# Eleven gate/up tiles by seven products, in pairs, with two weight sums made by accumulating transfers

## The chip, the cores and the metric

The kernel runs on one core of a Trainium2 chip. The metric is the time of one execution in device microseconds; the kernel before takes 910.9 us (median of three runs, 910.83 to 911.63). The engines are named as the profile names them: PE (TensorE, matrix products), PEld (its weight loads), DVE (VectorE), ACT (ScalarE), POOL (GpSimd) and SP (SyncE, which issues transfers here).

## The reference

One encoder layer over 512 positions of width 1024, in float32: a layer norm, two attention branches and their output projection, a memory cross-attention, and a convolutional gated linear unit, each followed by a layer norm. The change lies in the last of these:

```python
def conv_glu(h, w_gate, w_up, conv_w, conv_b, w_down):
    s = h.shape[1]
    g = h @ w_gate                       # (512, 1024) @ (1024, 2816)
    half = CONV_WIDTH // 2               # CONV_WIDTH = 3
    gp = jnp.pad(g, ((0, 0), (half, half), (0, 0)))
    g = sum(gp[:, j:j + s] * conv_w[j] for j in range(CONV_WIDTH)) + conv_b
    return (jax.nn.gelu(g, approximate=False) * (h @ w_up)) @ w_down
```

## The kernel before

Every matrix product in the kernel is made of three in a reduced format: each float32 operand is split into a rounded part, hi (an ACT cast), and the remainder, lo (a DVE subtraction), and hi·hi, hi·lo and lo·hi are summed in PSUM.

**The gate/up stage.** The 2816 columns of w_gate and w_up are cut into 22 tiles of 128 columns. A tile f yields 128 features of the gate and 128 of the up projection for all 512 positions. The activations h2T lie transposed, 8 blocks of 128 along the contraction. Tiles 0 and 1 are computed while the stage before ends. From tile 2 on there are two kinds:

- An *ordinary* tile loads the two 512 KB weight tiles (`w_cols`, L144), splits each into hi and lo, and runs `gemm_fm` (L170) twice: 2 x 8 x 3 matmuls of 128x512, gate into a PSUM tile g, up into s.
- A *seven-product* tile (`seven`, L1424; the tiles named in SEVEN, L52) takes gate and up together as a 2x2 block matrix, with gate and up as its rows and the two halves of the contraction as its columns (a11, a12 of the gate; a21, a22 of up), and the activations as four quarters B11 to B22 (contraction halves by halves of the positions). In Winograd's form of Strassen's method it needs seven products of blocks in place of eight: 7 x 4 x 3 = 84 matmuls of 128x256. For this it makes four sums of weight blocks on DVE (s1 to s4, L1433 to L1437), four remainders and as many casts (`parts`, L1417), and puts the products together afterwards with one ACT copy and four DVE additions (L1458 to L1462). The sums of the activations' quarters (T, by `t_forms`, L1388) are made once, during tiles 2 to 4.

`ffn_tail` (L1350) then applies the convolution's three taps, the Gelu and the product with up, into act[f]. After tile 21 the down projection runs over act.

**Buffers.** Weights as loaded lie in "raw" (3 buffers of 512 KB). s1 and s3 share one tile, s2 and s4 another, of "gb" (2 buffers). hi and lo have 6 buffers each; a seven-product tile takes four of each, an ordinary one two. A seven-product tile's output is put together in gu, which has 1 buffer. In PSUM, t and o have one buffer each (tile f's first product goes into o for odd f, into t for even f), g and s two each; a seven-product tile takes both g and one s, an ordinary one one g and one s.

**Order.** On PE the matmuls of this stage are issued in the order of the program text (`tc.manual_schedule`, L1466); on the other engines a planner places the instructions by a simulation of their times, and each engine's queue then runs in that order. Weight loads are issued by SP. Before the change POOL issues no transfers; in this stage it has nothing to do.

Seven-product tiles are 5, 7, 9, 11, 13, 15, 17 and 19, so that an ordinary tile stands behind each.

Of the kernel before, what the change touches and what calls it, by code (L numbers as in the profile page):

```python
# [9 lines left out]
F32 = mybir.dt.float32  # L10
# [3 lines left out]
ALU = mybir.AluOpType  # L14
# [3 lines left out]
P = 128  # L18
D = 1024
S = 512  # L20
NB = S // P
KD = D // P
# [26 lines left out]
]  # L49

MEM_AT = (2, 0)
SEVEN = (5, 7, 9, 11, 13, 15, 17, 19)  # L52
WARM = (12, 3)
CI, CF, CS, CMA, CM1, CM3 = 0, 128, 129, 130, 514, 770
CW = 898
# [17 lines left out]
def hymba_layer(ctx: ExitStack, tc: tile.TileContext, A, cst_d, out):  # L73
    nc = tc.nc
    X = mybir.AxisListType.X

    def pool(name, bufs=1, side="left", space=None):
        kw = {} if space is None else {"space": space}
        if space is None:
            kw["side"] = side  # L80
        return tc.tile_pool(name=name, bufs=bufs, **kw)

    cpool = ctx.enter_context(pool("const", side="right"))
    wpool = ctx.enter_context(pool("weights", side="right"))
# [110 lines left out]
    def ps_tile(tag, bufs, shape=None):  # L195
        return gpool.tile(shape or [P, 512], F32, tag=tag, bufs=bufs, name=tag)

    def g_tile():
        return ps_tile("g", 2)

    def s_tile():
        return ps_tile("s", 2, [P, 2, 512])
# [1123 lines left out]
    act = fp.tile([P, NF, S], F32, name="act")  # L1326
# [20 lines left out]
        for i in range(4):  # L1347
            pre_gemm(i, 1)

    def ffn_tail(f, pg, pu):  # L1350
        c = fp.tile([P, S], F32, tag="c", bufs=3, name="c")
        nc.scalar.activation(c, pg, AF.Identity, scale=cwT[:, 22 + f : 23 + f], bias=cwT[:, 66 + f : 67 + f])
        nc.vector.scalar_tensor_tensor(
            c[:, 1:S], pg[:, 0 : S - 1], cwT[:, f : f + 1], c[:, 1:S], ALU.mult, ALU.add
        )
        nc.vector.scalar_tensor_tensor(
            c[:, 0 : S - 1], pg[:, 1:S], cwT[:, 44 + f : 45 + f], c[:, 0 : S - 1], ALU.mult, ALU.add
        )
        nc.scalar.activation(c, c, AF.Gelu)
        nc.vector.tensor_tensor(act[:, f, :], c, pu, ALU.mult)  # L1360

    HT, HK = S // 2, KD // 2
# [4 lines left out]
    R12, R22 = (raw_u[:, HK * i : HK * (i + 1), sr] for i in range(2))  # L1369
# [3 lines left out]
    def two_k(v, i):  # L1373
        return v[:, 2 * i : 2 * i + 2]

    def t_parts(n, i, r):
        if n < 3:
            hl = [xpool.tile([P, 2, HT], F32R, tag="x", bufs=12, name="x") for _ in range(2)]
        else:
            hl = [two_k(t4, i), cpool.tile([P, 2, HT], F32R, tag="rope", bufs=2, name="t4l")]  # L1380
        nc.scalar.copy(hl[0], r)
        nc.vector.tensor_tensor(hl[1], r, hl[0].bitcast(F32), ALU.subtract)
        T.setdefault(n, []).append(hl)

    def t_tile():
        return fp.tile([P, 2, HT], F32, tag="c", bufs=3, name="r")

    def t_forms(j):  # L1388

        if j == 2:  # L1390
            for i in range(2):
                r = t_tile()
                nc.vector.tensor_tensor(r, two_k(R22, i), two_k(R12, i), ALU.subtract)
                t_parts(2, i, r)
            return
        r, q = t_tile(), t_tile()
        for t, B in ((r, B11), (q, B21)):
            nc.vector.tensor_tensor(t, two_k(B[0], j).bitcast(F32), two_k(B[1], j).bitcast(F32), ALU.add)
        nc.vector.tensor_tensor(r, two_k(R12, j), r, ALU.subtract)
        t_parts(0, j, r)  # L1400
        nc.vector.tensor_tensor(r, two_k(R22, j), r, ALU.subtract)
        t_parts(1, j, r)
        nc.vector.tensor_tensor(q, q, r, ALU.subtract)
        t_parts(3, j, q)

    def moving(n):
        return lambda w, k: T[n][k // 2][w][:, k % 2, :]

    def quarter(q):
        return lambda w, k: q[w][:, k, :]  # L1410

    def product(ps, wt, u):
        for k in range(HK):
            for a, b in ((0, 0), (0, 1), (1, 0)):
                mm(ps, wt[a][:, k, :], u(b, k), k + a + b == 0, k == HK - 1 and a == 1)

    def parts(raw, n):  # L1417
        hi = wpool.tile([P, n, P], F32R, tag="hi", bufs=6, name="hi")
        nc.scalar.copy(hi, raw)
        lo = wpool.tile([P, n, P], F32R, tag="lo", bufs=6, name="lo")  # L1420
        nc.vector.tensor_tensor(lo, raw, hi.bitcast(F32), ALU.subtract)
        return [[t[:, HK * i : HK * (i + 1), :] for t in (hi, lo)] for i in range(n // HK)]

    def seven(f):  # L1424
        raw = []
        for name in ("w_gate", "w_up"):
            raw.append(wpool.tile([P, KD, P], F32, tag="raw", bufs=3, name="raw"))
            nc.sync.dma_start(raw[-1], A[name][0].rearrange("(k p) f -> p k f", p=P)[:, :, f * P : (f + 1) * P])
        a11, a12, a21, a22 = (t[:, HK * i : HK * (i + 1), :] for t in raw for i in range(2))
        s13, s24 = (wpool.tile([P, KD, P], F32, tag="gb", bufs=2, name="gb") for _ in range(2))  # L1430
        s1, s3, s2, s4 = (t[:, HK * i : HK * (i + 1), :] for t in (s13, s24) for i in range(2))
        A11, A12 = parts(raw[0], KD)
        nc.vector.tensor_tensor(s1, a21, a22, ALU.add)  # L1433
        nc.vector.tensor_tensor(s3, a11, a21, ALU.subtract)
        S1, S3 = parts(s13, KD)
        nc.vector.tensor_tensor(s2, s1, a11, ALU.subtract)
        nc.vector.tensor_tensor(s4, a12, s2, ALU.subtract)  # L1437
        S2, S4 = parts(s24, KD)
        (A22,) = parts(a22, HK)
        p1_ = ps_tile(("t", "o")[f % 2], 1)[:, sl]  # L1440
        product(p1_, A11, quarter(B11))
        two = [g_tile(), g_tile(), s_tile()[:, 0, :]]
        product(two[0][:, sl], A12, quarter(B21))
        product(two[1][:, sl], S1, moving(0))
        product(two[1][:, sr], S3, moving(2))
        product(two[0][:, sr], S2, moving(1))
        product(two[2][:, sl], S4, quarter(B22))
        product(two[2][:, sr], A22, moving(3))
        gu = fp.tile([P, 2 * S], F32, tag="gu", bufs=1, name="gu")
        u34 = act[:, f, :]  # L1450

        def twice(v):
            return v.unsqueeze(1).to_broadcast([P, 2, HT])

        def pair(v):
            return v.rearrange("p (a t) -> p a t", a=2)

        nc.scalar.copy(gu[:, S + HT :], p1_)  # L1458
        nc.vector.tensor_tensor(pair(gu[:, 0:S]), pair(two[0]), twice(gu[:, S + HT :]), ALU.add)
        nc.vector.tensor_tensor(pair(u34), pair(two[1]), twice(gu[:, sr]), ALU.add)  # L1460
        nc.vector.tensor_tensor(gu[:, S + HT :], two[1][:, sl], u34[:, sr], ALU.add)
        nc.vector.tensor_tensor(gu[:, HT : S + HT], two[2], u34, ALU.add)  # L1462
        ffn_tail(f, gu[:, 0:S], gu[:, S:])

    pin()
    with tc.manual_schedule(engines={nc.tensor.engine}):  # L1466
        for f in range(2):
            ffn_tail(f, pre[2 * f][1], pre[2 * f + 1][1])
        for f in range(2, NF):
            if f in SEVEN:  # L1470
                seven(f)
                continue
            wg = w_cols(A["w_gate"][0], f * P)
            wu = w_cols(A["w_up"][0], f * P)
            pg = g_tile()
            pu = s_tile()[:, 0, :]
            gemm_fm(pg, wg, h2T, 0, S)
            gemm_fm(pu, wu, h2T, 0, S)
            ffn_tail(f, pg, pu)
            if f < 5:  # L1480
                t_forms(f - 2)
# [78 lines left out]
```

## Time and profile before

| | |
|---|---|
| median of 3 runs | 910.9 us (910.83 to 911.63) |
| profiled execution, its own time | 911.27 us |
| its span, first to last instruction | 909.5 us |
| mean granted clock of TensorE | 0.998 |
| gate/up tiles 5 to 21 | 603.4 to 782.1 us of the span |
| HBM read / written | 87.82 MB / 4.19 MB |

The profile is of one execution. Busy times are sums of instruction durations per engine; matmuls overlap their neighbours, so that a matmul of 128x512 shows 0.39 us while the next starts 0.23 us after it. In the groups of instructions a row names line, engine, operation, output<-inputs and shapes; behind the bar stand the busy time, the mean of one in ns, and the idle time of the engine just before them with what ended it. In the timeline a row begins with its start and duration in us.

### The profile page before, as it was taken

To read this page: it belongs to the slowest core of one execution; us is meant where nothing else is said; L and a number is where in the kernel's file an instruction comes from. 1 tells how busy PE (TensorE), PEld (TensorE's weight loads), DVE (VectorE), ACT (ScalarE), POOL (GpSimd) and SP (SyncE) were. 2 spreads that over 40 slices of the span, in tenths; PEclk is the share of its full clock that TensorE was granted. 3 is DMA by queue.
4 is the path that set the end of the run, shared out by engine and by line. 5 is a ranking of instruction groups with operands and counts; after the bars stand their busy time and mean duration, and the time that the engine had idled before them with its cause. 6 is when DMAs were issued, how large, how long until landed. Compare 5 with 4: busy or idle time off the path is not lost.

```text
span 909.5 us, 12905 instructions
## 1 busy us (share of the span) xinstructions
PE 896.6 (99%) x5097; PEld 768.3 (84%) x5097; DVE 560.2 (62%) x956; ACT 385.0 (42%) x672; POOL 127.2 (14%) x106
## 2 busy tenths in 40 slices
PE   9999999999999999999999999999999999999996
PEld 7778987898878798788988889799999999888885
DVE  7975146335446667869466576877777767433346
ACT  4563436415545576315454224344444345222210
POOL 1064033431443420010000010000000000000001
PEclk9999999999999999999999999999999999999999
DMA  6762041214221337316222304233333354223201
GB/s 220 225 213 70 24 139 47 73 67 117 70 70 47 93 117 233 138 46 171 85 70 70 93 25 129 82 93 93 95 114 94 96 160 140 93 93 103 83 23 70
DMA packets 116942, 92.84 MB, mean 102 GB/s; under 512 B 12472, under 2 KB 100752, under 8 KB 116882
## 3 DMA queue, kind: packets, MB, share of 16 engines
q1 hardware_dynamic: 116048, 89.80, 32.4%
q10 hardware_dynamic: 834, 2.22, 0.6%
q8 instruction: 40, 0.66, 0.3%
q14 instruction: 20, 0.16, 0.1%
HBM read 87.82 MB, written 4.19 MB: 101 GB/s over the span
## 4 chain that ended last, share of the span: by engine, by line
PE 95%; DVE 3%; ACT 1%; DMA 1%; issue 0%; POOL 0%; DVEq 0%; ACTq 0%
PE g L168 54%; PE s L168 24%; PE o L168 5%; PE t L168 4%; PE o L694 3%; PE s L682 2%; PE s L208 1%; DMA vt<-in_ln_in_g_dram 1%; PE s L1225 0%; DVE lo L282 0%; DVE oA L348 0%; DVE st L312 0%; DVE Tlo L367 0%; POOL zs L530 0%; DVE mx L1206 0%
## 5 line engine op out<-in xcount | busy, mean ns | idle before, releaser
L138 DVE TENSOR_TENSOR lo<-raw,hi 128x1024 fp32r<-128x1024 f32 x126 | 157.2, 1249 | 86.6 <-ACT hi L136 85.9
L136 ACT CAST hi<-raw 128x1024 fp32r<-128x1024 f32 x126 | 132.3, 1051 | 141.5 <-PE g L168 92.5
L168 PE MATMUL g<-Thi,hi 128*128 128x512 f32 x240 | 94.8, 395 | 0.0
L168 PE MATMUL g<-Tlo,hi 128*128 128x512 f32 x240 | 94.2, 393 | 0.0
L168 PE MATMUL g<-Thi,lo 128*128 128x512 f32 x240 | 94.0, 392 | 0.0
L109 POOL TENSOR_TENSOR rs<-ve,mhalf 128x1 f32<-128x1 f32 x18 | 15.3, 852 | 524.9 <-DVE ve L115 513.6
L530 POOL TENSOR_TENSOR zs<-zs,rsn 128x512 f32<-128x512 f32 x29 | 59.2, 2040 | 147.5 <-DVE zs L529 147.5
L168 PE MATMUL g<-Uhi,hi 128*128 128x512 f32 (+1 forms) x224 | 77.5, 346 | 1.0 <-ACT hi L136 1.0
L168 PE MATMUL g<-Ulo,hi 128*128 128x512 f32 (+1 forms) x224 | 77.1, 344 | 0.0
L168 PE MATMUL g<-Uhi,lo 128*128 128x512 f32 (+1 forms) x224 | 77.0, 344 | 0.0
L168 PE MATMUL g<-hi,Thi 128*128 128x512 f32 x184 | 71.6, 399 | 0.0
L168 PE MATMUL g<-hi,Tlo 128*128 128x512 f32 x184 | 70.9, 395 | 0.5 <-DVE Tlo L1173 0.5
L168 PE MATMUL g<-lo,Thi 128*128 128x512 f32 x184 | 70.7, 395 | 0.4 <-DVE lo L282 0.4
L528 DVE TENSOR_TENSOR zs<-g,rc 128x512 f32<-128x512 f32 x29 | 20.0, 689 | 68.2 <-PE g L168 31.6
L168 PE MATMUL g<-x,hi 128*128 128x256 f32 x320 | 58.8, 284 | 0.0
L168 PEld LDWEIGHTS g<-Thi,hi 128*128 128x128 f32 x240 | 45.1, 188 | 11.1 <-issue 0.9
L168 PEld LDWEIGHTS g<-Tlo,hi 128*128 128x128 f32 x240 | 45.1, 188 | 10.3 <-issue 1.4
L168 PEld LDWEIGHTS g<-Thi,lo 128*128 128x128 f32 x240 | 45.1, 188 | 9.3
L168 PEld LDWEIGHTS g<-x,hi 128*128 128x128 f32 x320 | 50.0, 192 | 0.5 <-issue 0.3
L168 PEld LDWEIGHTS g<-hi,Tlo 128*128 128x128 f32 x184 | 42.2, 230 | 6.4 <-DVE Tlo L1173 1.0
L168 PEld LDWEIGHTS g<-Uhi,hi 128*128 128x128 f32 x224 | 42.5, 190 | 5.8 <-ACT hi L136 1.2
L138 DVE TENSOR_TENSOR lo<-act,hi 128x512 fp32r<-128x512 f32 x22 | 14.8, 690 | 52.8 <-ACT hi L136 52.8
(363 smaller groups left out, 2091.8 us busy)
## 6 DMA issues: line engine op xcount, KB each, us to landing
raw<-in_w_in_dram SPq DMA_DIRECT2D x37, 512.0 KB, 3.8
raw<-in_w_gate_dram SPq DMA_DIRECT2D x22, 512.0 KB, 3.8
raw<-in_w_up_dram SPq DMA_DIRECT2D x22, 512.0 KB, 3.9
raw<-in_w_down_dram SPq DMA_DIRECT2D x22, 512.0 KB, 3.4
raw<-in_w_xk_dram SPq DMA_DIRECT2D x8, 512.0 KB, 3.9
raw<-in_w_xv_dram SPq DMA_DIRECT2D x8, 512.0 KB, 3.5
raw<-in_w_xq_dram SPq DMA_DIRECT2D x8, 512.0 KB, 4.6
raw<-in_w_xo_dram SPq DMA_DIRECT2D x8, 512.0 KB, 3.5
```

The source lines that it names most:

```text
L109: nc.gpsimd.tensor_tensor(out_, in_, mhalf, ALU.pow)
L136: nc.scalar.copy(hi, raw)
L138: (eng or nc.vector).tensor_tensor(lo, raw, hi.bitcast(F32), ALU.subtract)
L168: on_pe(nc.tensor.matmul(o, l, r, start=first, stop=last))
L208: on_pe(nc.tensor.transpose(ps[:, i // 4, f : f + P], t[:, i * P : (i + 1) * P], ident))
L528: nc.vector.tensor_tensor(zc, ps, rc, ALU.mult)
L530: nc.gpsimd.tensor_tensor(sh, sh, rsn, ALU.mult)
L682: nc.tensor.transpose(tp[:, k, :], s_, ident)
L694: nc.tensor.matmul(o[HJ[j], t0:t1], lhs(j), rhs(j), start=i == 0, stop=i == len(parts) - 1)
```

## The change

Eleven tiles become seven-product tiles: 5, 7, 8, 10, 11, 13, 14, 16, 17, 19 and 20. Five pairs of them stand one behind the other.

In such a tile two of the four weight sums are no longer made on DVE. SP loads a quarter (4 blocks of 128x128, 256 KB) straight into the place of s1 and another into that of s3, and POOL issues a transfer for each that adds the first half of w_up onto it in memory (`accum_op=ALU.add`): s1 = a22 + a21, s3 = a11 + a21. The whole raw tiles of gate and up are loaded as before; the half a21 of the raw up tile is then not used. [...]

```diff
-SEVEN = (5, 7, 9, 11, 13, 15, 17, 19)
+SEVEN = (5, 7, 8, 10, 11, 13, 14, 16, 17, 19, 20)
...
-    def ffn_tail(f, pg, pu):
+    def ffn_tail(f, pg, pu, sign=1):
...
-        nc.vector.tensor_tensor(act[:, f, :], c, pu, ALU.mult)
+        if sign == 1:
+            nc.vector.tensor_tensor(act[:, f, :], c, pu, ALU.mult)
+        else:
+            nc.vector.scalar_tensor_tensor(act[:, f, :], c, -1.0, pu, ALU.mult, ALU.mult)
...
-        nc.vector.tensor_tensor(r, two_k(R12, j), r, ALU.subtract)
+        nc.vector.tensor_tensor(r, r, two_k(R12, j), ALU.subtract)
         t_parts(0, j, r)
-        nc.vector.tensor_tensor(r, two_k(R22, j), r, ALU.subtract)
+        nc.vector.scalar_tensor_tensor(r, r, -1.0, two_k(R22, j), ALU.mult, ALU.subtract)
         t_parts(1, j, r)
-        nc.vector.tensor_tensor(q, q, r, ALU.subtract)
+        nc.vector.scalar_tensor_tensor(q, r, -1.0, q, ALU.mult, ALU.subtract)
         t_parts(3, j, q)
...
     def seven(f):
+        s13, s24 = (wpool.tile([P, KD, P], F32, tag="gb", bufs=2, name="gb") for _ in range(2))
+        s1, s3, s2, s4 = (t[:, HK * i : HK * (i + 1), :] for t in (s13, s24) for i in range(2))
+
+        def rows_of(name, i):
+            return A[name][0].rearrange("(k p) f -> p k f", p=P)[:, HK * i : HK * (i + 1), f * P : (f + 1) * P]
+
+        for t, name, i in ((s1, "w_up", 1), (s3, "w_gate", 0)):
+            nc.sync.dma_start(t, rows_of(name, i))
+            nc.gpsimd.dma_start(t, rows_of("w_up", 0), accum_op=ALU.add)
         raw = []
...
-        a11, a12, a21, a22 = (t[:, HK * i : HK * (i + 1), :] for t in raw for i in range(2))
-        s13, s24 = (wpool.tile([P, KD, P], F32, tag="gb", bufs=2, name="gb") for _ in range(2))
-        s1, s3, s2, s4 = (t[:, HK * i : HK * (i + 1), :] for t in (s13, s24) for i in range(2))
+        a11, a12, _, a22 = (t[:, HK * i : HK * (i + 1), :] for t in raw for i in range(2))
         A11, A12 = parts(raw[0], KD)
-        nc.vector.tensor_tensor(s1, a21, a22, ALU.add)
-        nc.vector.tensor_tensor(s3, a11, a21, ALU.subtract)
+        nc.vector.tensor_tensor(s2, s1, a11, ALU.add)
+        nc.vector.tensor_tensor(s4, a12, s2, ALU.add)
         S1, S3 = parts(s13, KD)
-        nc.vector.tensor_tensor(s2, s1, a11, ALU.subtract)
-        nc.vector.tensor_tensor(s4, a12, s2, ALU.subtract)
         S2, S4 = parts(s24, KD)
...
-        ffn_tail(f, gu[:, 0:S], gu[:, S:])
+        ffn_tail(f, gu[:, 0:S], gu[:, S:], -1)
```

## The prediction

> **What bounds the kernel now.** I read the page first: its busy times, then its chain of work.
>
> ```profile
> span 909.5 us, 12905 instructions
> ...
> PE 896.6 (99%) x5097; PEld 768.3 (84%) x5097; DVE 560.2 (62%) x956; ACT 385.0 (42%) x672; POOL 127.2 (14%) x106
> ...
> PE 95%; DVE 3%; ACT 1%; DMA 1%; issue 0%; POOL 0%; DVEq 0%; ACTq 0%
> ```
>
> TensorE is busy for 99% of the span and makes 95% of the chain that ended last. A busy PE is not PE at its peak, so the next view is who PE waited for, from 556 us (the end of the stage before) to the end of the span. Its only row is one wait of 1.0 us, before any seven-product tile:
>
> ```profile
> PE g L168 <- ACT hi L136: 1.0, 1, 1.0
> ```
>
> So in the gate/up stage matmuls follow one another without a gap, and the stage is as long as its matmuls. What one tile costs is read from the chain in order of time, over one seven-product tile (tile 7: its matmuls into o, g, s) and the ordinary tile 8 behind it (into g, s), and from the windows over the same two tiles. A window row gives busy times of PE, weight load, DVE, ACT and POOL, then granted clock, DMA share and GB/s.
>
> ```profile
> 624.53 1.43 PE o L168 x12
> 625.97 5.76 PE g L168 x48
> 631.73 2.88 PE s L168 x24
> 634.61 5.47 PE g L168 x24
> 640.08 5.44 PE s L168 x24
> 645.51 0.12 PE o L168
> 624.37:634.45 10.08, 10.08 (x86) 10.07 (x85) 8.16 (x11) 4.56 (x5) 0.00 (x0) 1.00 0.37 106
> 634.45:645.35 10.90, 10.90 (x50) 9.01 (x49) 7.31 (x10) 4.45 (x7) 0.00 (x0) 1.00 0.32 96
> ```
>
> Tile 7 runs from 624.53 to 634.61, 10.08 us; tile 8 from there to 645.51, 10.90 us. The granted clock is 1.00 in both. DVE has 8.16 of 10.08 and 7.31 of 10.90 us, 74% of the two. It is the engine nearest to becoming a bound.
>
> **The change part by part.**
>
> *Three more tiles in seven products.* SEVEN grows from 8 to 11 of the 17 tiles from 5 to 21. Each swap replaces 10.90 us of matmuls by 10.08 us: 0.82 us, times 3 = 2.46 us. This lies wholly on the path. It is the only gain there is, since everything else that the change removes is DVE time, for which PE does not wait today.
>
> *Pairs.* Until now an ordinary tile, light on DVE, stood behind every seven-product tile. Now two heavy tiles stand together five times (7-8 to 19-20), then one ordinary tile. So the DVE bill of such a tile decides. These are groups of instructions (count, busy us, mean ns, then idle before them) between 603.39 and 782 us, and last ACT's copy in the view of the tile gu (min, median and max ns):
>
> ```profile
> L1433 DVE TENSOR_TENSOR gb<-raw 128x512 f32<-128x512 f32 x7 | 4.8, 692 | 15.3 <-DMA raw<-in_w_up_dram 15.3
> L1436 DVE TENSOR_TENSOR gb<-gb,raw 128x512 f32<-128x512 f32 x7 | 4.8, 685 | 0.0
> L1434 DVE TENSOR_TENSOR gb<-raw 128x512 f32<-128x512 f32 x7 | 4.8, 684 | 0.0
> L1437 DVE TENSOR_TENSOR gb<-raw,gb 128x512 f32<-128x512 f32 x7 | 4.8, 684 | 0.0
> L138 DVE TENSOR_TENSOR lo<-raw,hi 128x1024 fp32r<-128x1024 f32 x22 | 26.8, 1222 | 13.0 <-ACT hi L136 12.9
> L1421 DVE TENSOR_TENSOR lo<-gb,hi 128x1024 fp32r<-128x1024 f32 x14 | 17.2, 1226 | 8.7 <-ACT hi L1419 8.7
> L1421 DVE TENSOR_TENSOR lo<-raw,hi 128x512 fp32r<-128x512 f32 x7 | 4.8, 681 | 0.0
> L1459 DVE TENSOR_TENSOR gu<-g,gu 128x512 f32<-128x512 f32 x8 | 5.5, 683 | 0.0
> L1460 DVE TENSOR_TENSOR act<-g,gu 128x512 f32<-128x512 f32 x8 | 5.5, 691 | 0.2
> L1461 DVE TENSOR_TENSOR gu<-g,act 128x256 f32<-128x256 f32 x8 | 3.3, 417 | 0.0
> L1462 DVE TENSOR_TENSOR gu<-s,act 128x512 f32<-128x512 f32 x8 | 5.4, 681 | 0.0
> L1353 DVE SCALAR_TENSOR_TENSOR c<-gu,cwT,c 128x511 f32<-128x511 f32 x8 | 6.0, 751 | 3.0 <-ACT c L1352 3.0
> L1360 DVE TENSOR_TENSOR act<-c,gu 128x512 f32<-128x512 f32 x8 | 5.5, 691 | 5.3 <-ACT c L1359 5.3
> L1458 ACT COPY gu<-o x8: 372/372/373, 605.0 to 751.9; 128x256 f32<-128x256 f32 x8
> ```
>
> Per seven-product tile: four weight sums, 0.69 + 0.68 + 0.69 + 0.68 = 2.74; three whole remainders (lo) of 1.22 or 1.23 and a half one of 0.68, 4.35; four recombinations, 0.68 + 0.69 + 0.42 + 0.68 = 2.47; two taps of 0.75 and the product 0.69, 2.19. Together 11.75 us, more than the tile's 10.08. The change takes L1433 and L1434 away (-1.38) and turns the last product into the form of L1353 (0.75 for 0.69, +0.06): 10.43 us. An ordinary tile costs 2 x 1.22 + 2 x 0.75 + 0.69 = 4.63. Three tiles cost 2 x 10.43 + 4.63 = 25.5 of 31.06 us, 82%; without the accumulating transfers it would be 91%. So DVE keeps up over a period, if not inside a pair; what carries a pair is that weights are made ahead. Two of the three sign changes in the prepared forms of the activations also go from 0.69 to 0.75, four instructions in tiles 2 and 3, 0.24 us; PE has no wait on DVE there, so I cost them at nothing (uncovered: 0.24).
>
> *Handover inside a pair.* gu has one buffer: tile 8's first recombination needs ACT's copy into it, which waits for tile 7's last reader, L1360. Tile 7's end on DVE today:
>
> ```profile
> 635.31 0.42 DVE L1461 TENSOR_TENSOR gu<-g,act 128x256 f32<-128x256 f32 x1
> 635.65 0.68 DVE L1462 TENSOR_TENSOR gu<-s,act 128x512 f32<-128x512 f32 x1
> 636.25 0.68 DVE L1421 TENSOR_TENSOR lo<-raw,hi 128x512 fp32r<-128x512 f32 x1
> 639.51 0.69 DVE L1360 TENSOR_TENSOR act<-c,gu 128x512 f32<-128x512 f32 x1 [0.76 <-ACT c L1359]
> ```
>
> L1360 ends at 640.20, 5.59 us into the next tile. Add the copy (0.37) and L1459 (0.68): 6.64. The deadline is the tile behind the pair, which writes that g buffer at 10.08. Spare: 3.4 us. Queued in front on DVE today, from the start of tile 8, are one whole and one half remainder (1.9). In a pair, as the six hi/lo buffers come free, it would be at most three whole ones and two sums (3 x 1.22 + 2 x 0.69 = 5.0), 3.1 more. It just fits, so I take nothing. The other deadline, L1461 of tile 7 before tile 8's third product (2.88 us in, at 637.49 on this clock), has 1.8 us to spare over its end at 635.73.
>
> *Accumulating transfers.* Each seven-product tile gets two plain 256 KB loads on SP and two accumulating 256 KB transfers on POOL. POOL's queue is empty there: its last instruction before the stage and the first after it are the rows below. The trace shows no accumulating transfer and none issued by POOL, so its time is bounded.
>
> ```profile
> raw<-in_w_up_dram SPq DMA_DIRECT2D x14, 512.0 KB, 3.9
> gb<-in_ln_g_dram SPq DMA_DIRECT2D x1, 512.0 KB, 5.2
> 552.04 0.92 POOL L109 TENSOR_TENSOR rs<-ve,mhalf 128x1 f32<-128x1 f32 x1 [11.27 <-DVE ve L115]
> 880.57 0.91 POOL L109 TENSOR_TENSOR rs<-ve,mhalf 128x1 f32<-128x1 f32 x1 [327.61 <-DVE ve L115]
> L530 POOL TENSOR_TENSOR zs<-zs,rsn 128x512 f32<-128x512 f32 x29 | 59.2, 2040 | 147.5 <-DVE zs L529 147.5
> 621.25 0.37 SPq L1428 DMA_DIRECT2D raw<-in_w_up_dram  x1
> ```
>
> Below: 3.9 us, a plain load of twice the size. Above: two such loads (destination and source are both read) and 2.0 us of POOL's work, its dearest row, 9.8. I take 5.2, the slowest transfer into the same gb buffers. What can wait: for tile 10 the first load goes out when the buffer of tile 8's sums comes free, about 2.4 us into tile 7 (ACT cast and lo after tile 6 has ended). With 3.9 for the load, the sum is whole 6.3 us in plus the transfer. The add that reads it (L1436) holds what is behind it in DVE's queue, tile 7's L1462 to L1360 at worst: 4.55 us (635.65 to 640.20) which must end 9.0 into tile 8, so it must start by 14.5 us into tile 7; two adds before it leave 13.1. So a transfer may take 6.8 us at no cost; 5.2 costs nothing.
>
> The Trainium skill, "DMA: Bandwidth & Descriptors", section "Anatomy of one DMA — SWDGE (gpsimd) path", gives 2.0 us plus the bytes over 436 GB/s for a transfer issued by GpSimd; for 256 KB that is an estimate of 2.6 us, and by it the sum would stay at -2.46. No run here shows it yet.
>
> SP issues four transfers where it issued two, 0.37 us each, and a load that waits for a gb buffer holds the raw loads behind it. The row of 621.25 is for tile 9, which starts at 645.51: 24 us ahead, so a few us there cost nothing. The DMA engines: 0.37 of 10.08 us is 3.7 us per tile now; half as much again for the two plain loads and as much once or twice over for the two accumulating ones make 7.4 to 9.3, and 18 to 22 of 31 us over three tiles. No limit.
>
> Sum: -2.46 us. The profiled execution took 911.27 us, of which the span is 909.5; it would become 908.8. The median shown is 910.9, 0.37 lower, so **908.4**.
>
> **The rivals.**
>
> *Handover pays* (chance 0.28). If DVE also waits for ACT between the remainders put in front (today it idles 0.3 to 1.0 us before one), 3.1 becomes 3.4 to 4.1 against 3.4 spare, some 0.4 us in each of five pairs: +2.0, 910.4. For: DVE's 10.43 us in a 10.08 us tile. Against: the chain of L1462 to L1360 has its own gaps, in which remainders fit. A new POOL queue that adds up to the 1.8 us that now lie outside the span ends here too. Bounds 909.1 to 912.7.
>
> *The accumulating transfer is late* (0.18). It decides from 6.8 us on. Each us beyond stops PE in four places (a pair with a pair to come), break-even 2.46 / 4 = 0.6, at 7.4. At 9.8 it is 3.0 x 4 = 12 us, 920.4; halfway, at 8.3, 6 us, 914.4. For: DVE already stands still for a plain load in the row of L1433, 15.3 us in 7 times. Against: 24 us of lead.
>
> *POOL's issue is held off by DVE* (0.04). Today DVE runs without a gap from 604.08 to 609.45:
>
> ```profile
> 604.08 0.69 DVE L1433 TENSOR_TENSOR gb<-raw 128x512 f32<-128x512 f32 x1 [1.32 <-DMA raw<-in_w_up_dram]
> 608.23 1.22 DVE L1421 TENSOR_TENSOR lo<-raw,hi 128x1024 fp32r<-128x1024 f32 x1
> ```
>
> An issue that waited for such a stretch would take 5.2 + 5.4 = 10.6 us, 3.8 late, four times: +15, 923.6. Nothing in this profile shows POOL held off, and POOL has no instruction in the stage that could; the small chance is for what cannot be seen. The Trainium skill, "SBUF — State Buffer", section "SBUF: two separate sides", says that VectorE in a two-port mode keeps GpSimd from writing descriptors, and names copies, not tensor_tensor, as what does so. The groups quoted for this stage are TENSOR_TENSOR and SCALAR_TENSOR_TENSOR alone; whether POOL's issues suffer from them no run here shows.
>
> *The swap saves nothing* (0.04): two sevens in a row run longer than 2 x 10.08 on PE itself. That gives 910.9 or so. Against: the matmuls and their shapes are the same as in tile 7.
>
> **How the numbers follow.** About 0.2%, 1.8 us, is what a measurement of this kernel can tell from no change: faster is below 909.1, slower above 912.7. The forecast has 0.46 (its own range 907.8 to 909.0), all of it faster. Handover and no saving, 0.32, are the same; late and held off, 0.22, slower. The range is 907.8 to 915.0: it leaves out the upper half of the late transfers, the held-off case and a little below, some 0.17.
>
> **What would show it.** Right: tile starts 10.08 apart in pairs, three tiles in 31.06 us, PE with no wait from tile 5 on, L1433 and L1434 gone from DVE and POOL's transfers under 6.8 us. Wrong: PE waiting at the first matmul into g behind a pair for L1459 or L1461 (handover); DVE idle before the add in L1436's place for longer than the 2.2 us of today (15.3 in 7) with a gb transfer as releaser (late); POOL's issue as long as a DVE stretch (held off). A wait of PE on a hi or lo tile inside a pair would mean that DVE does not keep up with the weights after all, and that the 82% was the wrong sum.

## The result: 924.9 us, slower by 1.5%, and the profile after

The changed kernel takes 924.91 us (median of five runs, 923.69 to 928.29), beside 911.09 us for the kernel before on the same chip: a ratio of 1.0154, interval 1.0143 to 1.0165. The forecast was 908.4 us with a range up to 915.0. The profiled execution took 925.44 us, its span is 923.6, 14.1 us more than before.

First the page of the changed kernel (busy times by engine, the chain's shares), then who PE waited for, from 540 us on (us in total, times, longest):

```profile
span 923.6 us, 13249 instructions
...
PE 900.3 (97%) x5205; PEld 775.5 (84%) x5205; DVE 566.9 (61%) x964; ACT 388.6 (42%) x681; POOL 156.1 (17%) x128
...
PE 84%; DVE 6%; DMA 5%; issue 2%; ACT 2%; POOL 1%; DVEq 0%; ACTq 0%; POOLq 0%
```
```profile
PE g L168 <- DVE gu L1468: 8.2, 4, 2.4
PE g L168 <- DVE c L1356: 2.7, 2, 1.9
```

PE fell from 95% to 84% of the chain; DVE and DMA took its place. L1468 is the first recombination of a seven-product tile (L1459 before): four waits, one behind each pair that has another pair to come. L1356 is a tap of `ffn_tail`. Neither was a wait of PE before.

Where the 14.1 us lie is read from windows over tiles 5 to 20, from the first matmul of tile 5 to the first one behind tile 20 (us, PE, PEld, DVE, ACT, POOL, granted clock, DMA share, GB/s). First before, then after:

```profile
603.39:771.23 167.84, 167.84 (x1057) 152.70 (x1056) 125.15 (x162) 75.46 (x95) 0.00 (x0) 1.00 0.38 113
```
```profile
606.07:784.76 178.69, 169.70 (x1166) 158.51 (x1164) 127.40 (x164) 77.68 (x102) 23.32 (x18) 0.98 0.66 156
...
627.05:638.18 11.13, 10.29 (x86) 10.12 (x84) 9.14 (x12) 6.15 (x9) 0.91 (x2) 1.00 0.42 120
638.18:650.85 12.67, 10.24 (x87) 10.07 (x85) 10.14 (x13) 6.32 (x8) 1.67 (x2) 1.00 0.95 212
650.85:663.41 12.56, 12.56 (x48) 10.26 (x49) 7.20 (x11) 3.06 (x4) 2.58 (x2) 0.86 0.54 100
```

The stage begins 2.7 us later (606.07 for 603.39), lasts 10.85 us longer (178.69 for 167.84), and what follows takes 0.6 us longer (138.84 for 138.27): 14.1 in all. The single rows are tiles 7 to 9. Tile 7 loses 1.05 us, most of it the second wait for L1356, 0.8. Tile 8, the second of a pair, takes 12.67: the 2.43 us wait at its end. Tile 9 takes 12.56 for 10.9 without any wait inside: its granted clock is 0.86. So there are three losses: an early one, the waits behind the pairs, and a clock that falls after some of them.

Now one such wait, on DVE's timeline from the end of tile 6 into tile 9 (start, duration, engine, line, operation, output<-inputs; in brackets the idle time before it and what ended it), and the matmul that waits:

```profile
625.05 0.69 DVE L1444 TENSOR_TENSOR gb<-gb,raw 128x512 f32<-128x512 f32 x1 [5.33 <-DMA gb<-in_w_up_dram]
...
632.47 2.45 DVE L1425 TENSOR_TENSOR lo<-gb,hi 128x1024 fp32r<-128x1024 f32 x2 [0.25 <-ACT hi L1423]
...
637.90 1.23 DVE L138 TENSOR_TENSOR lo<-raw,hi 128x1024 fp32r<-128x1024 f32 x1 [0.52 <-ACT hi L136]
...
641.63 0.69 DVE L1444 TENSOR_TENSOR gb<-gb,raw 128x512 f32<-128x512 f32 x1 [1.91 <-DMA gb<-in_w_up_dram]
642.24 1.22 DVE L138 TENSOR_TENSOR lo<-raw,hi 128x1024 fp32r<-128x1024 f32 x1
643.38 0.68 DVE L1445 TENSOR_TENSOR gb<-raw,gb 128x512 f32<-128x512 f32 x1
...
644.64 1.21 DVE L1425 TENSOR_TENSOR lo<-raw,hi 128x1024 fp32r<-128x1024 f32 x1
...
647.14 1.23 DVE L1425 TENSOR_TENSOR lo<-gb,hi 128x1024 fp32r<-128x1024 f32 x1 [0.62 <-ACT hi L1423]
648.28 0.68 DVE L1363 SCALAR_TENSOR_TENSOR act<-c,gu 128x512 f32<-128x512 f32 x1
648.88 1.22 DVE L1425 TENSOR_TENSOR lo<-gb,hi 128x1024 fp32r<-128x1024 f32 x1
650.02 0.68 DVE L1468 TENSOR_TENSOR gu<-g,gu 128x512 f32<-128x512 f32 x1
...
657.20 0.69 DVE L1444 TENSOR_TENSOR gb<-gb,raw 128x512 f32<-128x512 f32 x1 [4.25 <-DMA gb<-in_w_up_dram]
```
```profile
650.85 0.73 PE L168 MATMUL g<-Uhi,hi 128*128 128x512 f32 x1 [2.43 <-DVE gu L1468]
```

L1444 is the first sum that reads an accumulated tile. DVE stands 5.33 us in front of it for tile 8, 1.91 for tile 10 and 4.25 for tile 11, with everything behind it in the queue. Tile 8's matmuls end at about 648.3 (638.18 + 10.08); L1468 starts at 650.02, behind whole remainders of tiles 9 and 10 and the two sums of tile 10. Over the stage, DVE's waits and POOL's new line by its source (ns min/median/max of 22 issues; then us to landing) are these:

```profile
DVE gb L1444 <- DMA gb<-in_w_up_dram: 30.0, 9, 5.3
```
```profile
L1437 POOL DMA_DIRECT2D gb<-in_w_up_dram x22: 1273/1646/1862, 557.2 to 755.6; - x22
...
DMA to landing us min/median/max: 4.3/5.8/8.0
```

30.0 us in nine stands, 3.3 each. The transfers themselves, 5.8 us in the median, are hardly slower than the 5.2 us that the prediction took. They start late, as SP's queue shows (load of tile 10's sum, then of tile 11's):

```profile
633.72 0.37 SPq L1436 DMA_DIRECT2D gb<-in_w_up_dram  x1
...
648.39 0.37 SPq L1436 DMA_DIRECT2D gb<-in_w_up_dram  x1
```

633.72 is when tile 8's remainder of s13, in the two of 632.47, ends; 648.39 is when tile 10's (647.14 + 1.23 = 648.37) ends. One buffer holds s1 and s3 of all tiles, so a sum cannot begin to load until DVE has read the sum before it, and DVE then stands until load and addition are done: 7.9 us from issue to add for tile 10 (633.72 to 641.63), 8.8 for tile 11 (648.39 to 657.20).

### The profile page after: what moved, and what is told of

It is laid out like the page before. It is cut to its first block, busy times and chain, and to the rows that moved or that the text cites. A ratio compares the mean times of both kernels' runs of the same rounds, so it can differ in the third digit from the quotient of the medians.

```text
span 923.6 us, 13249 instructions
## 1 busy us (share of the span) xinstructions
PE 900.3 (97%) x5205; PEld 775.5 (84%) x5205; DVE 566.9 (61%) x964; ACT 388.6 (42%) x681; POOL 156.1 (17%) x128
## 3 DMA queue, kind: packets, MB, share of 16 engines
q0 software_dynamic: 11616, 5.77, 5.1%
## 4 chain that ended last, share of the span: by engine, by line
PE 84%; DVE 6%; DMA 5%; issue 2%; ACT 2%; POOL 1%; DVEq 0%; ACTq 0%; POOLq 0%
PE g L168 48%; PE s L168 20%; PE t L168 5%; PE o L168 4%; DMA gb<-in_w_up_dram 4%; PE o L694 3%; PE s L682 2%; DVE lo L1425 1%; ACT hi L1423 1%; PE s L208 1%; DMA vt<-in_ln_in_g_dram 1%; DVE c L1356 0%; DVE gu L1468 0%; DMA raw<-in_w_gate_dram 0%; PE s L1225 0%
## 5 line engine op out<-in xcount | busy, mean ns | idle before, releaser
L138 DVE TENSOR_TENSOR lo<-raw,hi 128x1024 fp32r<-128x1024 f32 x120 | 149.9, 1250 | 78.2 <-ACT hi L136 77.6
L136 ACT CAST hi<-raw 128x1024 fp32r<-128x1024 f32 x120 | 125.9, 1050 | 139.3 <-PE g L168 86.7
L168 PE MATMUL g<-Uhi,hi 128*128 128x256 f32 (+1 forms) x212 | 74.0, 349 | 10.0 <-DVE gu L1468 8.2
L168 PE MATMUL g<-Ulo,hi 128*128 128x256 f32 (+1 forms) x212 | 72.9, 344 | 0.0
L168 PE MATMUL g<-x,hi 128*128 128x256 f32 x392 | 71.9, 284 | 0.8 <-DVE c L1356 0.8
L168 PE MATMUL g<-Uhi,lo 128*128 128x256 f32 (+1 forms) x212 | 72.6, 343 | 0.0
L168 PEld LDWEIGHTS g<-x,hi 128*128 128x128 f32 x392 | 61.2, 192 | 1.5 <-issue 1.4
L1437 POOL DMA_DIRECT2D gb<-in_w_up_dram x22 | 28.7, 1570 | 175.6 <-DVE act L1469 69.9
L168 PE MATMUL g<-x,lo 128*128 128x256 f32 x196 | 55.5, 283 | 0.0
```

The lines of the kernel that those rows point to most:

```text
L138: (eng or nc.vector).tensor_tensor(lo, raw, hi.bitcast(F32), ALU.subtract)
L168: on_pe(nc.tensor.matmul(o, l, r, start=first, stop=last))
L1437: nc.gpsimd.dma_start(t, rows_of("w_up", 0), accum_op=ALU.add)
```

## The experiments

Three theories stood at the start: W, DVE's in-order queue stands on the accumulating transfers; H, the single gu holds up the handover in a pair; P, pairs cost by themselves. In the expectations W is also called L (and L' where the wait stands directly ahead of the recombination); D says that the transfers slow everything else, Q that DVE's queue is too full in a pair whichever buffer is free, O that only the planner's order is at fault, and B that the sums' buffer is filled too late whoever reads it. Each run is compared with the kernel before on the same chip (911.0 to 911.3 us).

**pairs_sums.** The eleven tiles of the change, all sums on DVE as before, no new transfers.

```diff
 (kernel before)
-SEVEN = (5, 7, 9, 11, 13, 15, 17, 19)
+SEVEN = (5, 7, 8, 10, 11, 13, 14, 16, 17, 19, 20)
```

> The kernel before with the eleven tiles in pairs alone; all four weight sums stay on DVE, no accumulating transfers. Theory L (the first add that reads an accumulated sum stands in DVE's queue, waits there for the transfer, and the recombinations of the tile behind it come late): no such wait here, so 908.4 to 911. Rival P (two heavy tiles in a row are too much for DVE or for the one gu buffer, whatever makes the sums): DVE has even more work here, 11.75 us against 10.43, so it must be as slow as the changed kernel or slower, 922 to 932.

911.81 us (911.25 to 912.84), ratio 1.0011 (1.0002 to 1.0021). PE's waits, and windows over tiles 5 to 20:

```profile
PE g L168 <- DVE gu L1459: 2.0, 4, 0.6
```
```profile
602.72:771.15 168.43, 166.44 (x1166) 156.12 (x1165) 138.76 (x185) 80.24 (x102) 0.00 (x0) 1.00 0.37 107
```

This is just above what W said (908.4 to 911) and far below what P said (922 to 932). Without its transfers the change is no faster than before: the first recombination is 0.4 to 0.6 us late behind each of four pairs.

**acc_single and late5.** The changed kernel with the eight single tiles of before: transfers, no pairs. late5 also queues tile 5's first sum on DVE behind tile 1's last product.

```diff
 (changed kernel; acc_single)
-SEVEN = (5, 7, 8, 10, 11, 13, 14, 16, 17, 19, 20)
+SEVEN = (5, 7, 9, 11, 13, 15, 17, 19)
 (late5, besides; tails[f] is the last product of tile f, behind() adds an edge of order on the engine)
...
-        nc.vector.tensor_tensor(s2, s1, a11, ALU.add)
+        ins = nc.vector.tensor_tensor(s2, s1, a11, ALU.add)
+        if f == 5:
+            behind(ins, tails[1])
```

> The changed kernel with the old list of eight tiles, none of them side by side; the accumulating transfers stay. Theory L: the add still waits for its transfer, but an ordinary tile behind each gives 10.9 us of room, so the stalls at g in the pairs go; the stall before tile 2 and the slow clock behind it (2.7 us) stay: 912.5 to 914.5. Rival P: 911, since only pairs cost. Rival D (the transfers slow the rest by themselves, through DMA or POOL): above 916.

> The eight-tile list with the accumulating transfers (914 us), with one order added: the first sum of tile 5 on DVE stands behind the last product of tile 1. If the 2.7 us before tile 5 come from that sum, which waits in DVE's queue for a plain load ahead of tile 1's tail, they go: 910.5 to 911.8. If they come from the transfers themselves, it stays at 913 to 914.5.

acc_single: 913.85 us (911.57 to 913.97), 1.0023 (1.0012 to 1.0033). late5: 911.41 (910.63 to 911.94), 1.0001 (0.9992 to 1.0010). In both, a single tile and the ordinary one behind it take 20.98 us and PE waits for nothing from tile 5 on. DVE stands on accumulated tiles here too, 14.4 us in six waits of acc_single. So an accumulating transfer costs nothing where an ordinary tile follows. What is left is one place in front of tile 2. DVE there in the changed kernel, then before:

```profile
569.14 0.74 DVE L1353 SCALAR_TENSOR_TENSOR c<-g,cwT,c 128x511 f32<-128x511 f32 x1
570.22 0.69 DVE L1444 TENSOR_TENSOR gb<-gb,raw 128x512 f32<-128x512 f32 x1 [0.34 <-DMA raw<-in_w_gate_dram]
570.83 0.74 DVE L1356 SCALAR_TENSOR_TENSOR c<-g,cwT,c 128x511 f32<-128x511 f32 x1
```
```profile
568.96 0.74 DVE L1353 SCALAR_TENSOR_TENSOR c<-g,cwT,c 128x511 f32<-128x511 f32 x1
569.74 0.75 DVE L1356 SCALAR_TENSOR_TENSOR c<-g,cwT,c 128x511 f32<-128x511 f32 x1
```

Of the raw tiles, tile 5's first sum now needs only the gate's, and the planner puts it earlier, between the two taps of tile 1. PE waits 1.9 us for the second tap (L1356); before, it waited 1.0 us there, for a cast of ACT. Tile 2 then runs at a lower clock, here in acc_single:

```profile
571.61:582.50 10.89, 10.89 (x41) 8.80 (x42) 6.64 (x10) 2.81 (x4) 0.00 (x0) 0.84 0.24 69
```

With the sum moved back (late5), tile 5 starts at 602.69 in place of 605.99, and the median is 2.4 us lower.

**no_acc.** The changed kernel without the 22 accumulating transfers (s1 and s3 lack their second term).

```diff
 (changed kernel)
             nc.sync.dma_start(t, rows_of(name, i))
-            nc.gpsimd.dma_start(t, rows_of("w_up", 0), accum_op=ALU.add)
```

> The changed kernel without the 22 accumulating transfers on POOL (they are left out, so two of the weight sums lack a term); the plain loads into the sums' tiles, the order of DVE and the pairs stay. Theory L: the add waits 3.5 us after the load is issued in place of 8 to 11, so the four stalls of 1.5 to 2.4 us at g vanish and the slow clock behind them; the 2.7 us before tile 5 stay, since there the add waits for a plain load: 910 to 913. Rival P: 918 or more.

918.65 us in one run: not the 910 to 913 of theory L, but what rival P said (918 or more), 6.3 us below the changed kernel. PE's waits, the window over tiles 5 to 20, and the end of tile 8 on ACT and on DVE:

```profile
PE g L168 <- DVE gu L1467: 6.1, 4, 1.5
```
```profile
605.98:778.43 172.45, 166.31 (x1165) 156.13 (x1164) 126.59 (x164) 78.78 (x102) 0.00 (x0) 1.00 0.46 134
```
```profile
645.75 1.05 ACT L1423 CAST hi<-gb 128x1024 fp32r<-128x1024 f32 x1 [1.26 <-PE s L168]
646.71 0.37 ACT L1466 COPY gu<-t 128x256 f32<-128x256 f32 x1
```
```profile
646.84 1.23 DVE L1425 TENSOR_TENSOR lo<-gb,hi 128x1024 fp32r<-128x1024 f32 x1 [1.00 <-ACT hi L1423]
647.98 0.68 DVE L1467 TENSOR_TENSOR gu<-g,gu 128x512 f32<-128x512 f32 x1
```

No DVE wait for gb is left, yet each pair still costs 1.5 us. The last whole remainder of tile 10 stands before tile 8's recombination on DVE, and its cast before the copy on ACT; the cast waits 1.26 us for a hi buffer that PE's s product of tile 8 still reads. (The 2.6 us before tile 5 are still there, 605.98 for 603.39.) This is what P comes to: an order that puts the next pair's preparation first hangs the recombination on PE's own progress.

**pool_plain.** The same transfers on POOL, plain, overwriting (again s1 and s3 lack a term): 

```diff
-            nc.gpsimd.dma_start(t, rows_of("w_up", 0), accum_op=ALU.add)
+            nc.gpsimd.dma_start(t, rows_of("w_up", 0))
```

> The changed kernel with POOL's 22 transfers as plain ones (they overwrite in place of adding, so two of the weight sums lack a term). If the adding is what makes them slow, they land in 3 to 3.5 us, as SP's loads of the same size do, and the time comes near that without them, 918 to 920. If it is the way over POOL, they take 5 us or more again and the time is 922 to 926.

918.55 us in one run. Issue to landing, POOL's plain transfers, and SP's of the same size beside them:

```profile
gb<-in_w_up_dram POOLq DMA_DIRECT2D x18, 256.0 KB, 4.7
gb<-in_w_up_dram SPq DMA_DIRECT2D x9, 256.0 KB, 3.1
```
```profile
604.03:777.92 173.89, 166.57 (x1165) 156.20 (x1164) 127.95 (x165) 77.76 (x102) 13.39 (x18) 1.00 0.55 161
```

The addition costs about 1.1 us of the 5.8; most of the duration is there without it. The time fits the expectation for the adding (918 to 920), the duration is nearer to the one for POOL. That the time equals no_acc's is chance: tile 2 kept its clock here (tile 5 starts at 604.03 for 605.98), and tiles 5 to 20 (second fence) take 1.4 us more than in no_acc. They take 4.8 us less than in the changed kernel, although DVE, in the same order around tile 8, still stands 23.9 us in eight waits on gb. So the length of DVE's stands does not give their price; it depends on whether the recombination behind them comes later than PE. Here PE's four waits for it were 1.5 to 2.2 us long, and no clock fell behind them.

**ordered.** The first sum of tile f on DVE behind the last product of tile f-2, so that no product stands behind a DMA.

```diff
 (changed kernel)
...
-        nc.vector.tensor_tensor(s2, s1, a11, ALU.add)
+        behind(nc.vector.tensor_tensor(s2, s1, a11, ALU.add), tails[f - 2])
```

> The changed kernel with one order added: the first add that reads an accumulated sum (s2 of tile f) is queued on DVE behind the last product of tile f-2. Nothing else changes. Theory L: DVE no longer stands still with a tail behind it, neither before tile 2 nor in the pairs; PE's waits go and the time is 908 to 911. Rival P or D: it stays above 918, since DVE's work, the buffers and the transfers are the same.

937.66 us (935.87 to 942.87), 1.0300 (1.0267 to 1.0333), where 908 to 911 was expected: a miss. The sum also reads s1, so the later it runs the later its buffer comes free and the next load starts (tile 7's sum ends at 619.53, and the load for tile 8's goes out at 619.60). The wait moved into ACT's queue (first fence), where the copy into gu stands behind it, and PE waits longer (second):

```profile
ACT hi L1425 <- DMA gb<-in_w_up_dram: 61.8, 9, 9.2
```
```profile
PE g L168 <- DVE gu L1475: 24.1, 5, 6.9
```

**s2_raw.** s2 made from raw tiles by two DVE additions (a21 + a22, + a11), the transfers kept: DVE's sums read no accumulated tile.

```diff
 (changed kernel)
-        a11, a12, _, a22 = (t[:, HK * i : HK * (i + 1), :] for t in raw for i in range(2))
+        a11, a12, a21, a22 = (t[:, HK * i : HK * (i + 1), :] for t in raw for i in range(2))
...
-        nc.vector.tensor_tensor(s2, s1, a11, ALU.add)
+        nc.vector.tensor_tensor(s2, a21, a22, ALU.add)
+        nc.vector.tensor_tensor(s2, s2, a11, ALU.add)
```

> The changed kernel, but DVE makes s2 from the raw tiles (two additions in place of one) and so reads no accumulated sum before its cast; the accumulating transfers stay for s1 and s3. Theory W (what the transfers cost in the changed kernel is DVE standing still for them with a tail in its queue): DVE's 30 us of waits go; without any accumulating transfer the time was 918.7, and it comes to 913 to 919 although DVE has one addition more. Rival B (the buffer of the sums is filled too late in any case, so that the next engine in line, ACT's cast, waits in its place): 920 to 928, with ACT waiting for gb.

917.87 us (915.27 to 919.08), 1.0063 (1.0047 to 1.0078): 7.0 below the changed kernel and inside W's 913 to 919. In the profiles 2.6 us of it are the early place (tile 5 starts at 603.48 for 606.07, since the first sum needs the up tile again); tiles 5 to 20 take 174.96 for 178.69, with one fall of the clock (behind a wait of 3.55 us) in place of two. What DVE and PE wait for:

```profile
DVE gb L1444 <- DMA raw<-in_w_up_dram: 20.0, 9, 4.2
```
```profile
PE g L168 <- DVE gu L1469: 7.1, 4, 3.6
```

The stand on gb is gone, one on the raw up tile has come. So W holds for part of the loss; the waits behind the pairs remain.

**pairs_p1 and after_p1.** Theory H by itself: ACT copies the first product into a spare place of its own instead of gu, in pairs_sums and in the changed kernel.

```diff
...
-        nc.scalar.copy(gu[:, S + HT :], p1_)
-        nc.vector.tensor_tensor(pair(gu[:, 0:S]), pair(two[0]), twice(gu[:, S + HT :]), ALU.add)
+        p1c = cst[:, CMA + HT * (f % 2) : CMA + HT * (f % 2 + 1)]
+        nc.scalar.copy(p1c, p1_)
+        nc.vector.tensor_tensor(pair(gu[:, 0:S]), pair(two[0]), twice(p1c), ALU.add)
```

> The kernel before with the eleven tiles in pairs, sums on DVE, and ACT's copy of the first product put into a tile of its own (a part of the constants' tile that is no longer read) in place of gu, so that it need not wait for the last product of the tile before. Theory H (in a pair the handover through the one gu buffer is what is late: tile f's last product, ACT's copy, the first recombination): the four waits of 0.4 to 0.6 us at g go, 908.4 to 909.6. Rival Q (DVE's queue itself is too full in a pair, whichever buffer is free): the waits stay, 911 to 913.

> The changed kernel with the same copy in a tile of its own, all else as changed. Theory H: DVE still waits for the transfers, but the first recombination no longer hangs on the tail behind that wait; the four stalls at g shrink below 0.7 us and the clock is kept: 911 to 916, of which 2.7 are the stall before tile 2. Rival L' (the wait of DVE for the transfer stands ahead of the recombinations in DVE's own queue): above 920.

pairs_p1: 912.40 us (911.71 to 912.64), 1.0012 (1.0002 to 1.0021), as pairs_sums. PE's waits behind the pairs stay, three of the four now put down to a cast of the next pair (first fence). For sums on DVE, H falls: for tile 11 the copy starts at 668.30 (second fence, ACT) and the recombination that reads it at 676.62 (third, DVE), behind a remainder:

```profile
PE g L168 <- ACT hi L1419: 1.8, 3, 0.7
```
```profile
668.30 0.37 ACT L1459 COPY cst<-o 128x256 f32<-128x256 f32 x1 [0.51 <-PE o L168]
```
```profile
675.49 1.22 DVE L1421 TENSOR_TENSOR lo<-gb,hi 128x1024 fp32r<-128x1024 f32 x1
676.62 0.68 DVE L1460 TENSOR_TENSOR gu<-g,cst 128x512 f32<-128x512 f32 x1
```

after_p1: 918.81 us (917.24 to 921.87), 1.0087 (1.0067 to 1.0106), 6.1 below the changed kernel, between the two expectations (911 to 916, above 920). In its profile the clock stayed at 1.00 behind every wait, where the changed kernel lost it three times, 4.9 us in all; PE waits 5.8 us for the first recombination (L1469 here) in place of 8.2, and not at all in tile 7. DVE's order is another too: tile 8's recombination, at 646.29, now stands ahead of tile 10's last whole remainder, at 646.90. How much of the gain is the copy's place, how much the order and how much the clock's chance, no run separates.

**pairs_order, pairs_best, after_best, pairs_order5.** If DVE's order sets the price, one edge mends it: the remainders of s13 and s24 of the next pair's first tile go behind the first recombination of this pair's second tile. pairs_order is pairs_sums with that edge, pairs_best also has the own copy place, after_best is the changed kernel with edge, copy place and late5's edge. pairs_order5 is pairs_order again, in six runs.

```diff
 (pairs_sums; parts() queues its remainder on DVE behind `after`)
...
-        S1, S3 = parts(s13, KD)
+        after = firsts.get(f - 2) if f - 1 not in SEVEN and f - 3 in SEVEN else None
+        S1, S3 = parts(s13, KD, after)
...
-        S2, S4 = parts(s24, KD)
+        S2, S4 = parts(s24, KD, after)
...
-        nc.vector.tensor_tensor(pair(gu[:, 0:S]), pair(two[0]), twice(gu[:, S + HT :]), ALU.add)
+        firsts[f] = nc.vector.tensor_tensor(pair(gu[:, 0:S]), pair(two[0]), twice(gu[:, S + HT :]), ALU.add)
```

> The same order without the copy's own tile (the copy goes through gu). Theory O with gu as a second condition: the copy still waits for the last product of the tile before, so 0.3 to 0.6 us of wait stay at each pair: 910.5 to 912. If gu plays no part: 908.3 to 909.5.

> pairs_p1 (sums on DVE, the copy in a tile of its own) with one order added: in the second tile of a pair the remainders of the next pair's sums (lo of s13 and s24) are queued on DVE behind that tile's first recombination. Theory O (what is late in a pair is the first recombination, because the planner queues preparation ahead of it on a DVE that is full there): the four waits of PE go, 908.3 to 909.5. Rival Q (DVE has too much work in a pair in whatever order): the waits move to another place and the time stays at 911 to 913.

> The changed kernel with all three: the copy's own tile, that order, and the first sum of tile 5 behind tile 1's last product. Theory O and L together: the 2.7 us before tile 5 go, the recombination is no longer behind the preparation, and what is left is DVE's wait for the transfer where it stands ahead of the recombination: 908.5 to 912. If the accumulating transfers cost by themselves: above 914.

> pairs_order again, timed in rounds: the kernel before, eleven tiles in pairs, sums on DVE, and the one order on DVE. If the order alone is enough and gu plays no part: 908.3 to 909.3, the interval of the ratio wholly below 0.998. If its single look was lucky: 910 to 912.

pairs_order: 908.61 us in one run. pairs_best: 908.89 (908.38 to 909.60), 0.9974 (0.9964 to 0.9984). pairs_order5: 908.66 (908.08 to 908.83), 0.9970 (0.9959 to 0.9982), below both kernels; the upper end of its interval is just above the 0.998 that was expected. after_best: 914.31 (912.59 to 918.86), 1.0037 (1.0024 to 1.0049): not the 908.5 to 912 of O and L, but above 914, as expected if the transfers cost by themselves. Beside pairs_best, which has the same edge and copy place without the transfers, that cost is 5.4 us. DVE around tile 11's recombination, in pairs_sums and then in pairs_order5:

```profile
674.55 1.22 DVE L1421 TENSOR_TENSOR lo<-gb,hi 128x1024 fp32r<-128x1024 f32 x1
675.68 0.69 DVE L1459 TENSOR_TENSOR gu<-g,gu 128x512 f32<-128x512 f32 x1
```
```profile
673.66 0.68 DVE L1469 TENSOR_TENSOR gu<-g,gu 128x512 f32<-128x512 f32 x1
674.26 1.22 DVE L1428 TENSOR_TENSOR lo<-gb,hi 128x1024 fp32r<-128x1024 f32 x1
```

One remainder of 1.2 us has changed places with the recombination. PE's only wait in pairs_order5 from 540 us on, and its window over tiles 5 to 20:

```profile
PE g L168 <- ACT hi L136: 1.0, 1, 1.0
```
```profile
602.60:767.97 165.37, 165.37 (x1165) 155.90 (x1164) 137.62 (x185) 79.88 (x102) 0.00 (x0) 1.00 0.37 109
```

165.37 us, 2.47 below the 167.84 of before. DVE has 137.62 us of work in it, 10.2 more than in the changed kernel's 178.69: relieving DVE was not what pairs needed. In after_best tiles 5 to 20 take 168.98 us; DVE still stands 20.1 us in nine waits on the accumulated tiles, and PE waits twice for the recombination, 1.7 us together.

## Why the prediction was wrong, step by step

**Three more tiles in seven products, -2.46: right.** The swap is worth 2.47 us in pairs_order5, and the 908.66 us are what the forecast expected of a PE without waits.

**DVE keeps up over a period: right, and beside the point.** PE never waited for a weight's hi or lo in this stage of the changed kernel, and the 127.40 us of DVE in 178.69 leave much room. What counts is what stands in front of one instruction.

**Handover inside a pair, "at most three whole ones and two sums", 5.0 us: the step that failed first.** From 637.90, just ahead of tile 8's start, to L1468 there stood five whole remainders and two sums (5 x 1.22 + 2 x 0.69 = 7.5 us), with stands of 1.91 us for the transfer and 0.62 for ACT between them. The fifth needs a hi buffer that tile 8 itself frees near its end (its cast waits 1.26 us for it in no_acc). I bounded the queue by the buffers free at tile 8's start, and did not count those that come free during the tile. The rival that the handover pays had the right place, in part the right cause (remainders put in front) and, for sums on DVE, the right price (0.4 to 0.6 us a pair in pairs_sums, some 0.4 expected, though in four pairs and not five). The chain through gu, with which the working started, was not what ended last: pairs_p1 took gu away and nothing changed, pairs_order5 left it and moved one remainder. In nearly the changed kernel's order (the planner puts a sum or two elsewhere) the price is 1.5 us a pair even with no accumulating transfer (no_acc): tiles 5 to 20 take 172.45 us, 7.1 above pairs_order5.

**Accumulating transfer, free up to 6.8 us: the duration nearly right, its start wrong.** Load and addition were put at 3.9 + 5.2 = 9.1 us; 7.9 to 8.8 were measured. But the load of tile 10's sum was to go out 2.4 us into tile 7 and went 6.7 us in (633.72 - 627.05), because the remainder that frees its buffer had itself stood behind the 5.33 us for tile 8's sum. The add came 14.6 us into tile 7 (641.63) where 13.1 was the limit. Late sum, late remainder, late load, late sum: the buffer closes a loop through DVE's queue, and I had worked out one round of it from an undisturbed start. The transfers add 6.2 us to tiles 5 to 20 (178.69 - 172.45), half of it by the clock. Both signs that were named for these rivals came up: PE waits for L1468 behind the pairs, and DVE stands in front of the add with a gb transfer as releaser.

**The lower clock: not in the prediction.** Tiles 9 and 15 take 12.56 and 12.55 us in place of 10.9, 3.3 us, and tile 2 loses another 1.6 of the 2.7 us before tile 5: 4.9 of the 14.1 us. Without them the result would lie near the late transfer's 920.4. That 924.9 is near the 923.6 of a held-off POOL is chance: POOL's longest issue took 1.86 us.

**"PE has no wait on DVE there", the edits before tile 5 at nothing: wrong.** In the changed kernel the prepared sums of the activations change sign, and the up projection comes out negated, for which `ffn_tail`'s last product has a factor of -1. No wait of PE is put down to these instructions. But the first sum's inputs changed, the planner moved it ahead of a tap, PE waited 0.9 us longer there, and with the clock that fell behind the wait tile 5 started 2.7 us later. I costed the durations of the new instructions and not their new place.

**SP, POOL's issue, the DMA engines: mostly right.** POOL's issues took 1.27 to 1.86 us, not a DVE stretch. The DMA share over the stage was 0.66, inside the 18 to 22 of 31 us; 0.95 in tile 8. Whether that lengthened transfers there, no run separates.

Sum, in spans: -2.47 for the swap, 2.7 before tile 5, 7.1 for the order in pairs, 6.2 for the transfers, 0.6 behind the stage: 14.1. The 7.1 and the 6.2 rest on one run of no_acc, and the two parts are not independent: s2_raw, without the stand on gb, was 3.7 us shorter in these tiles, 1.6 of it by the clock; pool_plain, with 23.9 us of stands, was 4.8 us shorter. That the changed order and the transfers cost is shown; how the loss divides between the stands on the transfer and the clock that fell behind some waits is not.

What stays open: whether a third buffer for the sums would let the transfers fit a pair. No run tried it. So nothing here shows a pair with accumulating transfers that beats before.

## What to carry to other kernels

Handing an engine's work to a DMA relieves it only if what stands behind that DMA in its in-order queue can wait: with an ordinary tile behind each the stands cost nothing, in pairs they did. Follow the buffer's loop (last reader, load, addition, next reader) for several rounds, not one. Before making an overfull engine lighter, read what its queue holds in front of the one instruction that others wait for: here one edge of order was worth 3 us, and 10 us less DVE work was worth nothing. When an instruction loses an input, look where the planner now puts it.

## What the hardware showed that I had not expected

**Short waits of PE can cost the clock.** In the changed kernel, after the waits of 2.43 and 2.35 us behind tiles 8 and 14, and 1.89 before tile 2, the granted clock was 0.84 to 0.87 over the next tile and 1.6 to 1.7 us were lost each time; after 1.84 (behind tile 11) and 1.53 it stayed at 1.00. In no_acc it fell to 0.84 after 2.08 us before tile 2, yet in pool_plain it stayed at 1.00 after 2.00 there and 2.17 behind a pair. The duration alone doesn't decide it. The Trainium skill, "TensorE: Matmul & The Clock Gate", section "What's actually happening", says that the clock halves after an idle window of about 3.4 us, and that the window runs freely. One window at half the clock would lose an estimate of 1.7 us; the size agrees with the 1.6 to 1.7 measured. That a wait well under a window suffices is not what it says; here 1.89 us did. Where such a wait falls against the window could decide it, which no run here shows.

**Transfers issued by POOL.** 256 KB took 5.8 us accumulating, 4.7 plain, and 3.1 plain when SP issued them. For the same 5.77 MB POOL's queue carried 11616 packets accumulating and 1760 plain, and one issue took POOL 1.65 us against 0.75 (medians). The estimate of 2.6 us that the prediction drew from the Trainium skill, "DMA: Bandwidth & Descriptors", section "Anatomy of one DMA — SWDGE (gpsimd) path", is too short for both kinds that POOL issued.
